# A convolution gate that stays in PSUM, and an output bias added in four slices during the mixer

## The chip, the cores and the metric

The kernel runs on one core of a Trainium2 chip, in one launch. The metric is the device time of one execution in microseconds (us); the median over the runs counts. The engines named here are PE (TensorE; PEld is its weight load), DVE (VectorE), ACT (ScalarE), POOL (GpSimd) and SP (SyncE, which only issues DMAs here).

## The reference

A decoder trunk of two layers over 256 tokens with 2048 features, all in float32. Layer 0 mixes tokens with a Conformer convolution, layer 1 with a diagonal state-space model (SSM); each mixer is followed by an MLP with a squared ReLU, and a last RMSNorm ends it. What matters here is the convolution mixer:

```python
def conv_module(h, w_in, b_in, dw, dw_b, ln_g, ln_b, w_out, b_out):
    u = h @ w_in + b_in                      # 2048 -> 4096
    a, gate = jnp.split(u, 2, axis=-1)
    v = a * jax.nn.sigmoid(gate)
    v = depthwise_causal_conv(v, dw, 31 taps) + dw_b
    v = layer_norm(v, ln_g, ln_b)
    v = jax.nn.silu(v)
    return v @ w_out + b_out                 # added to the residual x
```

## The kernel before

Every matmul is done in float32 quality with rounded operands: a weight tile `raw` is split into `hi` (ACT, L117) and `lo = raw - hi` (L119), and products of high and low parts are added up in PSUM. One weight tile (a step) is split in two halves; `run_steps` splits four halves ahead of the one that PE consumes, out of four buffers each for `hi` and `lo`. In the mixer's first projection (`conv_in`) DVE makes the `lo` of the first steps and POOL all the others (`pool_lo`), because DVE has the convolution to do.

`conv_in` walks over 16 blocks `c` of 128 channels. For each, PE computes value and gate rows (feature-major, 128 x 256 each) in one PSUM accumulator of two banks (`acc`, two buffers), over two steps, that is four halves of 24 matmuls (L204 to L206). Then `gate(c, A)` makes three instructions: DVE multiplies both by the RMSNorm factor of each token (L424, result `ga` in SBUF), ACT takes the sigmoid of the second half in place (L425), and DVE adds the bias to the first half and multiplies (L426, result in `vT`, SBUF).

For blocks 0 to 11 the depthwise convolution follows on DVE: one tap after another, 30 instructions of the form `scalar_tensor_tensor` (L792) into the PSUM tile `cv`, the last into `vT`. Blocks 12 to 15 (`PACKED`) are convolved on PE instead: a DMA (for block 15 copies on ACT and DVE, L445 and L447) lays out shifted rows `R`, POOL multiplies out the tap matrix `wpk` (L376), and 32 matmuls (L463, tile `pk`) give the block. For the LayerNorm, groups of blocks are centred by a common shift (L543), squared on ACT (L545) and summed over channels by PE (`stat`, L510); `ln_totals` and `ln_finish` (L555 to L579) finish the sums after block 15.

`ln_finish` then normalises block pair by block pair: DVE subtracts and scales (L792, L604), ACT applies SiLU (L607) and rounds the high part `sT` (L230), and DVE makes its low part (L231, both inputs in SBUF). PE multiplies `sT` by `w_out` (`conv_out`, L215 to L217) as soon as the pairs are there. The residual `x` lies in SBUF token-major; `add_x` adds each finished slice of 512 columns of `w_out`'s product to it.

Before the first step of `conv_out`, its `pre` calls `ln_finish`, then fetches the output bias as one tile `bo` (one row broadcast to 128 partitions, L624, on POOL's DMA queue) and adds it to `x` with four POOL instructions (L627). After that come the SSM's background preparations (`ssm_prep`), which begin with loads of `bb` on the same queue.

The order on each engine is made by a scheduler that simulates the program's times; `tick` and `after(n, fn)` place a function n halves later in the program, and `behind(ins)` keeps an instruction behind another. Where the text speaks of an order, it is the order in the built program.

Of the kernel before, what the change touches and what calls it, by code (L numbers as in the profile page):

```python
# [9 lines left out]
F32 = mybir.dt.float32  # L10
F32R = mybir.dt.float32r
I32 = mybir.dt.int32
AF = mybir.ActivationFunctionType
ALU = mybir.AluOpType
# [4 lines left out]
P = 128  # L19
EPS = 1e-6  # L20
D = 2048
T = 256
KB = D // P
NB = T // P
NS = D // 512
# [11 lines left out]
class Trunk:  # L37
# [320 lines left out]
    def packed_taps(self):  # L358

        nc = self.nc  # L360
        n = len(PACKED)
        self.R = self.blk_tile([P, 3, 4, T + 28], name="R")
        self.wpk = self.blk_tile([P, n, 32, 32], name="wpk")

        def prep():
            dp = self.t2([P, n, 4, 8], name="dp")
            for r in range(4):
                for g in range(4):
                    nc.vector.tensor_copy(out=dp[32 * r:32 * r + 32, :, g, :],
                                          in_=self.dw[32 * g:32 * g + 32, PACKED[0]:, r::4])  # L370
            for i in range(n):
                self.after(1 + 8 * i, lambda i=i: block(dp[:, i], i))

        def block(dp, i):
            with self.behind(self.pool_ins):
                nc.gpsimd.tensor_tensor(  # L376
                    out=self.wpk[:, i], in0=dp.rearrange("p g q -> p (g q)").unsqueeze(2).broadcast_to([P, 32, 32]),
                    in1=self.m32.unsqueeze(1).broadcast_to([P, 32, 32]), op=ALU.mult)
        self.after(16, prep)

    def behind(self, ins):
        return self.tc.issue_after(getattr(ins, "ins", ins))
# [36 lines left out]
    def gate(self, c, A):  # L419
        nc = self.nc  # L420
        b_in = self.vec("b_in")
        t = self.tmp.tile([P, 2, T], F32, tag="ga", name="ga", bufs=2)
        with self.tc.high_priority(offset=URGENT):
            nc.vector.tensor_tensor(out=t, in0=A, in1=self.rstdB.broadcast_to([P, 2, T]), op=ALU.mult)  # L424
            nc.scalar.activation(t[:, 1, :], t[:, 1, :], AF.Sigmoid, bias=b_in[:, KB + c:KB + c + 1])  # L425
            nc.vector.scalar_tensor_tensor(out=self.cblk(c), in0=t[:, 0, :], scalar=b_in[:, c:c + 1], in1=t[:, 1, :],  # L426
                                           op0=ALU.add, op1=ALU.mult)
        if c in PACKED:
            self.depthwise_packed(c)
        else:  # L430
            self.depthwise(c)
# [183 lines left out]
    def conv_out(self):  # L615
        w = self.a["conv_w_out"][0]
        st = {}

        def pre():
            self.flush()  # L620
            self.ln_finish()
            self.rate = 2.75
            bo = self.blk_tile([P, D], name="bo")
            self.nc.gpsimd.dma_start(out=bo, in_=self.a["conv_b_out"].broadcast_to([P, D]))  # L624
            for n in range(NS):
                s = slice(n * 512, (n + 1) * 512)
                self.nc.gpsimd.tensor_tensor(out=self.x[:, :, s], in0=self.x[:, :, s],  # L627
                                             in1=bo[:, s].unsqueeze(1).broadcast_to([P, NB, 512]), op=ALU.add)
            self.ssm_prep()
        for n in range(NS):  # L630
            for kc in range(4):
                def consume(hi, lo, half, n=n, kc=kc):
                    if half == 0 and kc == 0:
                        st["acc"] = self.acc2()
                        if n == 0:
                            st["ssq"] = self.new_ssq()
                            self.new_hT()
                    k0 = (kc % 2) * 4 + half * 2
                    self.mm_t(st["acc"], lambda kk: self.sT[kc // 2][:, k0 + kk], hi, lo,
                              kc == 0 and half == 0, kc == 3 and half == 1)  # L640
                    if n == NS - 1 and kc == 2:
                        self.rate = 0
                    if kc == 3 and half == 1:
                        self.add_x(st["acc"], n)
                        self.feed(n, st["ssq"], "mlp0")
                if n == 0 and kc < 2:
                    self.pool_lo.add(len(self.steps))
                self.add_t(w, kc * 4, n * 512, consume, pre if n == 0 and kc == 0 else None)
# [811 lines left out]
```

## Time and profile before

| | us |
|---|---|
| median of 3 runs | 2077.03 |
| lowest, highest | 2071.52, 2077.48 |
| the profiled execution | 2073.18 |
| its span in the trace | 2071.4 |
| PE, DVE, ACT, POOL busy in it | 1996.2, 1426.4, 942.6, 304.4 |

The profile is that of one execution; all durations come from it. Its own time is 1.8 us over its span and 3.9 us under the median. Busy shares are averages over stages that differ: the mixer lies in the first 260 us, the first MLP and the SSM's preparations behind it. Matmuls are pipelined, so that "busy" for PE counts overlapping times, and the number of matmuls in a stretch says more. In the timelines a group's duration spans from its first start to its last end.

### The profile page before, as it was taken

The numbers are of one execution on the slowest core, as the hardware profiler recorded it, in microseconds if no ns is written. First come the engines' busy times: TensorE is split into PE (matmuls) and PEld (weight loads), VectorE is DVE, ScalarE is ACT, GpSimd is POOL, SyncE is SP. The second block draws the span as 40 slices with busy tenths as digits, with TensorE's granted clock in tenths as the row PEclk, the third lists the DMA queues.
The fourth block names the chain that finished last, engine by engine and source line by source line (L and its number), as shares of the span: only waits on it lengthen the run. The fifth ranks groups of instructions, "written<-read, shape, count | busy, mean of one in ns | idle before, by whom it ended". The sixth has DMA issues, their size and how long they took to land.

```text
span 2071.4 us, 28883 instructions
## 1 busy us (share of the span) xinstructions
PE 1996.2 (96%) x11612; PEld 1696.8 (82%) x11612; DVE 1426.4 (69%) x1897; ACT 942.6 (46%) x1155; POOL 304.4 (15%) x234
## 2 busy tenths in 40 slices
PE   8999798999999999999987799999999999999998
PEld 8899587788888888888876588888888888888887
DVE  7999899966767777776548635566565555655555
ACT  5444454454444545444433244455344444544444
POOL 2987401100000211111013410000000000000000
PEclk9999999999999999999997999999999999999999
DMA  8667367766856876667999975666566566565663
GB/s 230 164 176 209 108 201 246 229 216 189 266 185 188 220 217 214 202 213 225 254 299 222 216 234 184 192 184 193 184 189 197 183 189 197 183 211 192 186 192 133
DMA packets 330485, 420.09 MB, mean 203 GB/s; under 512 B 10081, under 2 KB 228241, under 8 KB 327889
## 3 DMA queue, kind: packets, MB, share of 16 engines
q1 hardware_dynamic: 316864, 384.86, 62.8%
q0 software_dynamic: 9488, 29.02, 4.7%
q10 hardware_dynamic: 4000, 4.38, 0.7%
q8 instruction: 91, 1.49, 0.3%
q14 instruction: 42, 0.34, 0.0%
HBM read 391.69 MB, written 26.53 MB: 202 GB/s over the span
## 4 chain that ended last, share of the span: by engine, by line
PE 79%; DVE 12%; DMA 4%; SPq 1%; issue 1%; ACT 1%; POOL 1%; ACTq 0%; POOLq 0%; DVEq 0%
PE acc L194 22%; PE acc L215 14%; PE acc L216 14%; PE acc L217 14%; PE acc L195 11%; DVE cv L792 6%; DMA raw<-in_ssm_w_glu_dram 2%; DVE lo L119 1%; SPq L91 1%; DVE vT L426 1%; DVE ws L783 1%; DMA raw<-in_mlp_w_down_dram 1%; DMA Vt<-Vd 0%; PE acc L204 0%; PE acc L205 0%
## 5 line engine op out<-in xcount | busy, mean ns | idle before, releaser
L117 ACT ACTIVATE hi<-raw 128x1024 fp32r<-128x1024 f32 x672 | 711.0, 1060 | 983.7 <-PE acc L217 480.0
L119 DVE TENSOR_TENSOR lo<-raw,hi 128x1024 fp32r<-128x1024 f32 x596 | 729.3, 1224 | 534.5 <-ACT hi L117 533.5
L194 PE MATMUL acc<-hT,hi 128*128 128x512 f32 x2048 | 726.5, 399 | 3.4 <-DVE t L771 3.4
L195 PE MATMUL acc<-hT,lo 128*128 128x256 f32 x2048 | 575.3, 281 | 3.3 <-DVE lo L119 3.3
L194 PEld LDWEIGHTS acc<-hT,hi 128*128 128x128 f32 x2048 | 385.3, 188 | 100.0 <-issue 3.2
L215 PE MATMUL acc<-hi,rT 128*128 128x512 f32 x992 | 388.6, 392 | 6.2 <-ACT hi L117 6.2
L195 PEld LDWEIGHTS acc<-hT,lo 128*128 128x128 f32 x2048 | 387.5, 189 | 4.8 <-DVE lo L119 3.9
L216 PE MATMUL acc<-lo,rT 128*128 128x512 f32 x992 | 387.4, 391 | 0.5 <-DVE lo L119 0.5
L217 PE MATMUL acc<-hi,rT 128*128 128x512 f32 x992 | 387.0, 390 | 0.0
L215 PEld LDWEIGHTS acc<-hi,rT 128*128 128x128 f32 x992 | 186.8, 188 | 47.2 <-ACT hi L117 6.6
L217 PEld LDWEIGHTS acc<-hi,rT 128*128 128x128 f32 x992 | 186.8, 188 | 39.5
L216 PEld LDWEIGHTS acc<-lo,rT 128*128 128x128 f32 x992 | 186.7, 188 | 39.0 <-DVE lo L119 1.0
L119 POOL TENSOR_TENSOR lo<-raw,hi 128x1024 fp32r<-128x1024 f32 x76 | 187.3, 2482 | 115.4 <-ACT hi L117 106.6
L204 PE MATMUL acc<-hT,hi 128*128 128x256 f32 x512 | 146.0, 285 | 1.5 <-ACT hi L117 1.5
L206 PE MATMUL acc<-hT,lo 128*128 128x256 f32 x512 | 145.4, 284 | 1.9 <-POOL lo L119 1.9
L205 PE MATMUL acc<-hT,hi 128*128 128x256 f32 x512 | 146.1, 286 | 0.2 <-DVE hT L252 0.2
L792 DVE SCALAR_TENSOR_TENSOR cv<-vT,dw,cv 128x256 f32<-128x256 f32 x348 | 142.1, 478 | 0.8
L217 PE MATMUL acc<-hi,yT 128*128 128x512 f32 x256 | 101.3, 396 | 8.1 <-DVE yT L231 8.1
L783 DVE TENSOR_TENSOR x<-x,acc 128x1024 f32<-128x1024 f32 (+1 forms) x72 | 83.6, 1161 | 33.3 <-PE acc L217 22.9
L204 PEld LDWEIGHTS acc<-hT,hi 128*128 128x128 f32 x512 | 98.5, 192 | 4.1 <-ACT hi L117 2.1
L215 PE MATMUL acc<-hi,yT 128*128 128x512 f32 x256 | 101.6, 397 | 0.0
L206 PEld LDWEIGHTS acc<-hT,lo 128*128 128x128 f32 x512 | 98.5, 192 | 3.0 <-POOL lo L119 2.1
(264 smaller groups left out, 1759.1 us busy)
## 6 DMA issues: line engine op xcount, KB each, us to landing
raw<-in_mlp_w_up_dram SPq DMA_DIRECT2D x128, 1024.0 KB, 5.8
raw<-in_mlp_w_down_dram SPq DMA_DIRECT2D x128, 1024.0 KB, 5.2
raw<-in_ssm_w_glu_dram SPq DMA_DIRECT2D x32, 1024.0 KB, 5.6
raw<-in_conv_w_in_dram SPq DMA_DIRECT2D x60, 512.0 KB, 5.5
raw<-in_conv_w_out_dram SPq DMA_DIRECT2D x16, 1024.0 KB, 5.3
Vd<-bv POOLq DMA_DIRECT2D x16, 512.0 KB, 5.0
Wt<-Wd SPq DMA_DIRECT2D x8, 1024.0 KB, 9.8
Mt<-Kd SPq DMA_DIRECT2D x32, 256.0 KB, 14.1
```

The costliest lines, as they stand in the source:

```text
L117: self.nc.scalar.activation(hi, sl, AF.Copy)
L119: ins = eng.tensor_tensor(out=lo, in0=sl, in1=hi.bitcast(F32), op=ALU.subtract)
L194: mm(accs[m], lhsT=hi[:, kk, c], rhs=x, start=first and kk == 0, stop=False)
L195: mm(accs[m][:, 0:T], lhsT=lo[:, kk, c], rhs=x[:, 0, :], start=False, stop=last and kk == 3)
L204: mm(accs[m], lhsT=hi[:, kk, c], rhs=x[:, 0, :], start=first and kk == 0, stop=False)
L205: mm(accs[m], lhsT=hi[:, kk, c], rhs=x[:, 1, :], start=False, stop=False)
L206: mm(accs[m], lhsT=lo[:, kk, c], rhs=x[:, 0, :], start=False, stop=last and kk == 3)
L215: mm(acc[:, b, :], lhsT=ak[:, 0, t], rhs=hi[:, kk, :], start=first and kk == 0, stop=False)
L216: mm(acc[:, b, :], lhsT=ak[:, 0, t], rhs=lo[:, kk, :], start=False, stop=False)
L217: self.mm_last = mm(acc[:, b, :], lhsT=ak[:, 1, t], rhs=hi[:, kk, :], start=False, stop=last and kk == 1)
L783: self.nc.vector.tensor_tensor(out=out, in0=a, in1=b, op=op)
L792: return self.nc.vector.scalar_tensor_tensor(out=out, in0=a, scalar=s, in1=b, op0=op0, op1=op1)
```

## The change

Two edits. In `gate`, the scaled product overwrites the accumulator `A` in PSUM; ACT's sigmoid reads it there and writes a tile `ga` of half the size in SBUF, and the last DVE instruction reads the value half from PSUM and the sigmoid from SBUF. The accumulator is then read until this last instruction. The second edit takes the bias out of `conv_out`'s `pre` and puts it into the mixer: at ticks 20, 28, 36 and 44 after the taps are set up, one slice of 512 columns of the bias is fetched (a tile from the pool `t2`) and added to `x` by POOL, behind the `lo` instruction last issued there.

```diff
@@ packed_taps
         self.after(16, prep)
+        for i in range(NS):
+            self.after(20 + 8 * i, lambda i=i: self.add_b_out(i))
+
+    def add_b_out(self, n):
+        nc = self.nc
+        s = slice(n * 512, (n + 1) * 512)
+        bo = self.t2([P, 512], name="bo")
+        nc.gpsimd.dma_start(out=bo, in_=self.a["conv_b_out"][:, s].broadcast_to([P, 512]))
+        with self.behind(self.pool_ins):
+            nc.gpsimd.tensor_tensor(out=self.x[:, :, s], in0=self.x[:, :, s],
+                                    in1=bo.unsqueeze(1).broadcast_to([P, NB, 512]), op=ALU.add)
@@ gate
-        t = self.tmp.tile([P, 2, T], F32, tag="ga", name="ga", bufs=2)
+        t = self.tmp.tile([P, T], F32, tag="ga", name="ga", bufs=2)
         with self.tc.high_priority(offset=URGENT):
-            nc.vector.tensor_tensor(out=t, in0=A, in1=self.rstdB.broadcast_to([P, 2, T]), op=ALU.mult)
-            nc.scalar.activation(t[:, 1, :], t[:, 1, :], AF.Sigmoid, bias=b_in[:, KB + c:KB + c + 1])
-            nc.vector.scalar_tensor_tensor(out=self.cblk(c), in0=t[:, 0, :], scalar=b_in[:, c:c + 1], in1=t[:, 1, :],
+            nc.vector.tensor_tensor(out=A, in0=A, in1=self.rstdB.broadcast_to([P, 2, T]), op=ALU.mult)
+            nc.scalar.activation(t, A[:, 1, :], AF.Sigmoid, bias=b_in[:, KB + c:KB + c + 1])
+            nc.vector.scalar_tensor_tensor(out=self.cblk(c), in0=A[:, 0, :], scalar=b_in[:, c:c + 1], in1=t,
                                            op0=ALU.add, op1=ALU.mult)
@@ conv_out, pre
             self.flush()
             self.ln_finish()
             self.rate = 2.75
-            bo = self.blk_tile([P, D], name="bo")
-            self.nc.gpsimd.dma_start(out=bo, in_=self.a["conv_b_out"].broadcast_to([P, D]))
-            for n in range(NS):
-                s = slice(n * 512, (n + 1) * 512)
-                self.nc.gpsimd.tensor_tensor(out=self.x[:, :, s], in0=self.x[:, :, s],
-                                             in1=bo[:, s].unsqueeze(1).broadcast_to([P, NB, 512]), op=ALU.add)
             self.ssm_prep()
```

On POOL, the stretch from the second tap matrix `wpk` (L376) to the first loads of the SSM's preparations stood like this before; `lo` (L119) is the low part of a weight half, `rstd` the LayerNorm's factor, `x` the residual:

```order
L376 TENSOR_TENSOR wpk<-dp,m_244 128x1024
L119 TENSOR_TENSOR lo<-raw,hi 128x1024 x8
L376 TENSOR_TENSOR wpk<-dp,m_244 128x1024
L119 TENSOR_TENSOR lo<-raw,hi 128x1024 x8
L376 TENSOR_TENSOR wpk<-dp,m_244 128x1024
L119 TENSOR_TENSOR lo<-raw,hi 128x1024 x24
L587 TENSOR_TENSOR rstd<-lv,mhalf 128x2
L624 DMA bo<-in_conv_b_out_dram 128x2048
L839 DMA bb<-in_ssm_b_re_dram 128x1024
L840 DMA bb<-in_ssm_b_im_dram 128x1024
L627 TENSOR_TENSOR x<-x,bo 128x2x512 x4
```

The same engine in the changed kernel, from the same `wpk` on, down to the last bias DMA:

```order
L376 TENSOR_TENSOR wpk<-dp,m_244 128x1024
L119 TENSOR_TENSOR lo<-raw,hi 128x1024 x3
L388 DMA bo<-in_conv_b_out_dram 128x512
L119 TENSOR_TENSOR lo<-raw,hi 128x1024 x2
L388 DMA bo<-in_conv_b_out_dram 128x512
L390 TENSOR_TENSOR x<-x,bo 128x2x512
L119 TENSOR_TENSOR lo<-raw,hi 128x1024 x2
L390 TENSOR_TENSOR x<-x,bo 128x2x512
L388 DMA bo<-in_conv_b_out_dram 128x512
L119 TENSOR_TENSOR lo<-raw,hi 128x1024
L376 TENSOR_TENSOR wpk<-dp,m_244 128x1024
```

The four DMAs and four additions now stand among the mixer's `lo` instructions (the last DMA follows after one more `lo`, the third addition after two more; the fourth after another five `lo`, the last `wpk` and three `lo`); behind `rstd` the loads of `bb` follow at once.

On DVE, the end of the mixer before, from the gate of the last block (L424) to the last packed block's result; `cv` and `vT<-vT,dw,cv` are taps, `R` the copies for block 15, `shift` the centring of a group:

```order
L424 TENSOR_TENSOR ga<-acc,bcs 128x512
L792 SCALAR_TENSOR_TENSOR cv<-vT,dw,cv 128x256 x3
L426 SCALAR_TENSOR_TENSOR vT<-ga,vecs 128x256
L792 SCALAR_TENSOR_TENSOR cv<-vT,dw,cv 128x256 x2
L447 COPY R<-vT 32x284 x6
L792 SCALAR_TENSOR_TENSOR cv<-vT,dw,cv 128x256 x6
L792 SCALAR_TENSOR_TENSOR vT<-vT,dw,cv 128x256
L792 SCALAR_TENSOR_TENSOR cv<-vT,dw,cv 128x256 x3
L543 TENSOR_TENSOR vT<-vT,shift 128x3x256
L792 SCALAR_TENSOR_TENSOR vT<-vT,dw,cv 128x256
L543 TENSOR_TENSOR vT<-vT,shift 128x4x256
L792 SCALAR_TENSOR_TENSOR vT<-pk_2827,vecs,shift 128x256
```

The same place in the changed kernel:

```order
L798 SCALAR_TENSOR_TENSOR cv<-vT,dw,cv 128x256 x18
L798 SCALAR_TENSOR_TENSOR vT<-vT,dw,cv 128x256
L798 SCALAR_TENSOR_TENSOR cv<-vT,dw,cv 128x256
L436 TENSOR_TENSOR acc<-acc,bcs 128x2x256
L798 SCALAR_TENSOR_TENSOR vT<-vT,dw,cv 128x256
L555 TENSOR_TENSOR vT<-vT,shift 128x4x256
L438 SCALAR_TENSOR_TENSOR vT<-acc,vecs,ga 128x256
L459 COPY R<-vT 32x284 x6
L555 TENSOR_TENSOR vT<-vT,shift 128x3x256
L798 SCALAR_TENSOR_TENSOR vT<-pk_2839,vecs,shift 128x256
```

Of the 16 instructions for taps that stood behind the last gate's first instruction, one is left, and the centring of four blocks stands ahead of the gate's last instruction. On PE, the sums of blocks 8 to 11 moved with it, in among the products of block 14.

## Rows read from the trace of the kernel before

**Rows 1.** The page's head: span, and busy time, share and number of instructions of each engine, and the group of the high parts (count | busy us, mean ns of one | idle before, cause).

```profile
span 2071.4 us, 28883 instructions
...
PE 1996.2 (96%) x11612; PEld 1696.8 (82%) x11612; DVE 1426.4 (69%) x1897; ACT 942.6 (46%) x1155; POOL 304.4 (15%) x234
...
L117 ACT ACTIVATE hi<-raw 128x1024 fp32r<-128x1024 f32 x672 | 711.0, 1060 | 983.7 <-PE acc L217 480.0
```

**Rows 2.** Busy time by stretch (from:to, length; busy us and instructions of PE, PEld, DVE, ACT, POOL; granted PE clock, DMA share, GB/s): the mixer's middle, its end with `conv_out`'s begin, and the stretch behind that.

```profile
100.00:200.00 100.00, 100.00 (x837) 97.22 (x836) 95.59 (x207) 44.71 (x52) 86.11 (x36) 1.00 0.68 182
200.00:300.00 100.00, 89.15 (x659) 69.43 (x658) 88.20 (x196) 50.49 (x83) 27.23 (x18) 0.95 0.50 158
300.00:400.00 100.00, 92.61 (x482) 77.52 (x481) 99.15 (x142) 47.24 (x61) 13.07 (x8) 0.98 0.75 231
```

**Rows 3.** DVE's timeline over one block of the mixer (start us, us, line, operation; in brackets idle time before and its cause).

```profile
152.74 0.68 DVE L424 TENSOR_TENSOR ga<-acc,bcs 128x512 f32<-128x512 f32 x1
153.34 1.76 DVE L792 SCALAR_TENSOR_TENSOR cv<-vT,dw,cv 128x256 f32<-128x256 f32 x4
155.01 1.50 DVE L426 SCALAR_TENSOR_TENSOR vT<-ga,vecs 128x256 f32<-128x256 f32 x1
156.43 7.92 DVE L792 SCALAR_TENSOR_TENSOR cv<-vT,dw,cv 128x256 f32<-128x256 f32 x20
164.27 0.68 DVE L424 TENSOR_TENSOR ga<-acc,bcs 128x512 f32<-128x512 f32 x1
```

**Rows 4.** DVE's instructions from 45 to 218 us by line and form (count | busy us, mean ns | idle before, cause), and the line L426 over the whole run (duration ns min/median/max, first and last start us).

```profile
L792 DVE SCALAR_TENSOR_TENSOR cv<-vT,dw,cv 128x256 f32<-128x256 f32 x334 | 135.9, 478 | 0.6
L426 DVE SCALAR_TENSOR_TENSOR vT<-ga,vecs 128x256 f32<-128x256 f32 x15 | 21.5, 1433 | 1.0 <-ACT ga L425 1.0
L792 DVE SCALAR_TENSOR_TENSOR vT<-vT,dw,cv 128x256 f32<-128x256 f32 x10 | 4.6, 472 | 0.0
...
L426 DVE SCALAR_TENSOR_TENSOR vT<-ga,vecs x16: 476/1548/2427, 33.4 to 217.9; 128x256 f32<-128x256 f32 x16
```

**Rows 5.** POOL's timeline, four places (columns as in rows 3): a tap matrix and a `lo` in the steady stretch, the bias DMA, and the four additions of the bias.

```profile
144.67 2.09 POOL L376 TENSOR_TENSOR wpk<-dp,m 128x1024 f32<-128x1024 f32 x1
...
156.68 2.41 POOL L119 TENSOR_TENSOR lo<-raw,hi 128x1024 fp32r<-128x1024 f32 x1 [0.45 <-ACT hi L117]
...
238.06 0.64 POOL L624 DMA_DIRECT2D bo<-in_conv_b_out_dram  x1
...
243.29 9.71 POOL L627 TENSOR_TENSOR x<-x,bo 128x1024 f32<-128x1024 f32 x4 [3.55 <-DMA bo<-in_conv_b_out_dram]
```

**Rows 6.** PE's timeline at the mixer's end: the last matmul of block 15, the products of blocks 13 and 14, those of block 15, the last channel sums, and the LayerNorm's totals.

```profile
215.29 0.28 PE L206 MATMUL acc<-hT,lo 128*128 128x256 f32 x1
215.50 7.11 PE L463 MATMUL pk<-R,wpk 128*32 128x256 f32 x128
223.84 4.38 PE L463 MATMUL pk<-R,wpk 128*32 128x256 f32 x64 [1.22 <-DVE R L447]
231.04 1.08 PE L510 MATMUL stat<-vT,ones 128*32 128x256 f32 x8 [2.82 <-DVE vT L543]
...
234.97 1.06 PE L561 MATMUL lst<-q,stat 128*128 128x1 f32 x8 [0.50 <-ACT stat L555]
```

**Rows 7.** DVE's timeline: a centring of four blocks in the mixer, and the mixer's end.

```profile
193.26 2.25 DVE L543 TENSOR_TENSOR vT<-vT,shift 128x1024 f32<-128x1024 f32 x1
...
216.11 0.68 DVE L424 TENSOR_TENSOR ga<-acc,bcs 128x512 f32<-128x512 f32 x1
...
217.89 2.09 DVE L426 SCALAR_TENSOR_TENSOR vT<-ga,vecs 128x256 f32<-128x256 f32 x1
...
220.69 3.34 DVE L447 COPY R<-vT 32x284 f32<-32x284 f32 x6
...
228.38 0.95 DVE L543 TENSOR_TENSOR vT<-vT,shift 128x768 f32<-128x768 f32 x1
...
229.75 1.23 DVE L543 TENSOR_TENSOR vT<-vT,shift 128x1024 f32<-128x1024 f32 x1
```

**Rows 8.** ACT's timeline at the mixer's end: the copies for block 15, a table load, and the result of block 14.

```profile
220.01 4.05 ACT L445 ACTIVATE R<-vT 32x284 f32<-32x284 f32 x9 [2.67 <-DVE vT L426]
...
225.03 1.28 ACT L449 ACT_TABLE_LOAD   x1
...
226.44 0.46 ACT L471 ACTIVATE vT<-pk,vecs 128x256 f32<-128x256 f32 x1
```

**Rows 9.** DVE's timeline in `ln_finish`: the low parts of `sT`, the first two pairs of instructions and a later single one.

```profile
243.59 4.86 DVE L231 TENSOR_TENSOR sT<-z,sT 128x256 fp32r<-128x256 f32 x2
...
250.76 3.40 DVE L231 TENSOR_TENSOR sT<-z,sT 128x512 fp32r<-128x512 f32 x2
...
257.01 0.68 DVE L231 TENSOR_TENSOR sT<-z,sT 128x512 fp32r<-128x512 f32 x1
```

**Rows 10.** PE's timeline at the begin of `conv_out`: two matmuls that waited for `sT`, one of the slow ones behind the last wait, and one after those.

```profile
245.99 0.50 PE L217 MATMUL acc<-hi,sT 128*128 128x512 f32 x1 [1.97 <-DVE sT L231]
...
253.62 0.50 PE L217 MATMUL acc<-hi,sT 128*128 128x512 f32 x1 [3.44 <-DVE sT L231]
...
255.73 0.63 PE L217 MATMUL acc<-hi,sT 128*128 128x512 f32 x1
...
258.73 0.39 PE L217 MATMUL acc<-hi,sT 128*128 128x512 f32 x1
```

## The prediction

> **What bounds the kernel now.** I read the page's head first: PE is busy for nearly the whole span, no other engine is near it [rows 1]. But busy shares average over stages, so the stretches come next [rows 2]. From 100 to 200 us PE gets 837 matmuls done and POOL and DVE are at 86 and 96 of 100 us; from 200 to 300 us PE gets only 659 done, and loses 10.9 us outright. So the change, which touches the mixer and its end, is worth what it does to that second stretch, unless it slows the first.
>
> In the mixer the gate's first instruction comes every 11.53 us (152.74, 164.27) [rows 3]: that is PE's pace, four halves of 2.88 us. DVE has no idle time there either, but its work is merely late: what it has not done when PE ends block 15 at 215.5 us is done afterwards. There the reader should follow PE [rows 6]: products of blocks 13 and 14 at once, those of 15 at 223.84 after its copies, then nothing until DVE's centring lets the sums begin at 231.04; the totals come at 234.97. Behind that, PE waits for the low parts of `sT`: the pairs that DVE starts at 243.59 and 250.76 take 4.86 and 3.40 us [rows 9], and PE's waits end at 245.99 and 253.62 [rows 10].
>
> **The gate.** The same instruction, 128 x 256, takes 1.43 us on average at L426 but 0.476 us at its fastest; taps of the same form and size, with one input in PSUM, take 0.478 and 0.472 us, however busy POOL is [rows 4]. What differs is that L426 has both inputs in SBUF while POOL, which reads SBUF, runs. The changed instruction has one in PSUM, so I price it like the taps: 0.47 us, or 0.40 from start to start (20 taps in 7.92 us [rows 3]). Over 15 gates DVE saves 15 x (1.43 - 0.47) = 14.4 us of duration. The first one now writes PSUM: a tap that writes PSUM costs 0.006 us more than one that writes SBUF [rows 4], so 0.1 us for 16. No row has such an output of 512 columns; bounds by the taps' difference scaled to size are 0 to 0.012 us each, by an outright second tap 0.47 us each, 7.5 us in all, and I take the first.
>
> The row of L426 shows no price of a PSUM input. The Trainium skill (Perfetto Trace Analysis, Optimizing Scalar/DVE Operations) gives VectorE some 60 ns of access overhead on SBUF and 125 ns on PSUM; by that the gate's two instructions would lose 16 x 2 x 65 ns = 2.1 us, an estimate from that page, all within the reserve worked out below. The trace does not agree: 0.472 us with PSUM, 0.476 without.
>
> The accumulator is held longer, from the first gate instruction's end to the last's, 155.01 + 1.50 - 153.42 = 3.1 us before [rows 3] and about 2 us after. PE needs that buffer again a whole block (11.5 us) later: hidden, unless DVE is 8 us late, when PE would lose the difference.
>
> **What the saving is worth.** Not 14 us: PE sets the pace up to 215.5 us. Until then DVE was some 16 taps late, 14 `cv` and two `vT` by the built order, 16 x 0.39 = 6.3 us. The nine gates from about 105 us on give back 9 x (1.55 - 0.40) = 10.4 us at L426's median [rows 4], so that DVE is up to date with about 4 us in reserve, as the built order has it (one tap left behind the last gate's first instruction). I lay out the new end with the old durations, from PE's end at 215.5:
> - gate 215.7 to 216.3, one tap, centring of four blocks 2.25 (POOL still runs; 1.23 when it does not) [rows 7] to 219.0, last gate instruction to 219.4;
> - ACT squares that group (128 x 1024 as for `hi`, 1.06 [rows 1]) and then makes ten copies (9 in 4.05 us, the tenth apart [rows 8]): to 224.4, so block 15's products start about 224, not earlier than now;
> - block 14's result follows a table load of 1.28 us, at 226.4 or a little before [rows 8]; but DVE is now free and centres its group at once, done at 227.5 instead of 229.3;
> - eight fewer sums of blocks 8 to 11 stand at the end. The rest of block 15's products and the last six sums end near 229.0, the totals follow at 229.5 instead of 234.97 [rows 6].
>
> Gain 5.4 us; between 3.5, if the copies come a us or two late, and 6.5.
>
> **The bias.** Before, the tile has landed 5.2 us after its issue (238.06 to 243.29) and POOL adds for 9.71 us from 243.29 to 253.0 [rows 5], exactly over both slow pairs of `sT`. These have two inputs in SBUF; a later one of twice the first ones' size takes 0.68 us [rows 9]. With POOL idle there the first pair costs 2 x 0.45 = 0.9 and the second 2 x 0.65 = 1.3: 4.0 + 2.1 = 6.1 us. PE's resumption moves with it: from 253.62 to about 247.5, before the gain of the stage ahead. Then the granted clock: behind the wait eight matmuls or so stand at 0.63 us against 0.39 later, 0.43 and 0.23 from start to start (255.73, 258.73 [rows 10]), the lower and the higher of the clock's two levels, after PE had waited 3.44 us. With shorter waits up to 8 x 0.2 = 1.6 us come back; I take 1.0, as the stretch behind is partly DVE's.
>
> On the row of `sT` the Trainium skill bears (SBUF — State Buffer, Who interferes with whom): a VectorE instruction with two SBUF inputs and a GpSimd instruction that reads SBUF exclude each other for the whole length of the one that started first. By that rule the pairs are slow only through POOL, the sum is -6.1; were they slow on their own account it would be 0, and the time that of the second rival. The trace agrees: L217's wait ends at 245.99, when the first addition of 2.43 us (243.29 + 2.43 = 245.72) is over. The rule also speaks against the change, because the additions now meet the mixer's centrings; these pay up to 2.43 us each, within the reserve.
>
> **What the bias costs where it is now.** POOL gets four additions of 9.71 / 4 = 2.43 us and four issues of 0.64 (the whole tile's; a quarter may be cheaper): 12.3 us, between two tap matrices of 2.09 us [rows 5], from about 105 to 165 us. Its reserve: a half lasts 2.88 us, a `lo` 2.41, so 0.47 per half, 9.4 us over 20 halves. That leaves 12.3 + 2 x 2.09 - 9.4 = 7.1 us of backlog. The buffers carry part: a half is split when the buffers four halves back come free, three halves (8.6 us) ahead of use; less 1.06 for `hi` [rows 1] and 2.41 for `lo`, 5.2 us. PE should lose 1 to 2 us, spread over two places; nothing if sums on PE give POOL room, and, as the upper bound, all 12.3 us if POOL had no reserve. I take 1.0. Behind a late `lo` on POOL's queue stand only further `lo`, tap matrices and bias slices; for the `lo` PE waits. The slices' DMAs bring the same 1 MB as before, at 182 GB/s of other traffic [rows 2], each two `lo` ahead of its addition: hidden if landing takes the 5.2 us of the whole tile. On that queue the loads of `bb` come about 6 us earlier. That costs nothing; DVE's two multiplications of `bb` move in front of the last low parts of `sT`, which still come about 1 us before PE needs them. Without that cover PE loses 1 us.
>
> **Sum.** -5.4 - 6.1 - 1.0 + 1.0 = -11.5 us. From 300 to 400 us DVE is full [rows 2], with the same work, begun as much earlier; I see nothing there that gives the gain back. Against the profiled execution's 2073.2 us that is 2061.7, against the median of the runs, 3.9 us higher, 2065.5. I forecast 2064, its own range 2057 to 2070.
>
> **Rivals.**
> 1. *POOL becomes the mixer's bound; slower.* Each addition waits for its slice on POOL's queue as the first did before (3.55 us [rows 5]), and nothing else runs there. Then 4 x 3.55 = 14.2 us join the 7.1 of backlog; less 5.2 that the buffers carry, PE loses 16 us and more when DVE's centrings hold POOL too. With 4 us of the tail's gain gone as well: -11.5 - 1.0 + 16 + 4 = +7.5, about 2083. It decides once POOL is over 5.2 us late. For it: POOL's 86 of 100 us. Against: two `lo`, 4.8 us, lie between most DMAs and their additions. 8%.
> 2. *Only one of the two gains comes.* The gate stays slow, or the copies for block 15 and block 14's result, whose times hardly move, set the end; or the `sT` pairs are slow for another reason. Then about -5 - 1 + 1 = -5 us: 2070. For it: the copies begin no earlier in my layout. Against: PE's empty 2.82 us before the sums [rows 6] are waited for DVE alone. 14%.
> 3. *The gain comes and is lost again* by 400 us, where DVE is 99% busy and the scheduler's order differs from before: 2074 to 2076, no change. Against: DVE's work is no larger, and it starts earlier. 12%.
>
> My forecast has the other 66%. A measurement here cannot tell less than 0.3%, about 6 us, from no change: below 2070.8 is faster. Of rival 2 half lies there, of the forecast nearly all: faster 0.71, same 0.21, slower 0.08. The range 2055 to 2075 holds the forecast, rival 2 and part of rival 3.
>
> **What would show it.** Right: the gate's last instruction at 0.47 us throughout; PE without gaps over 2 us in all from 100 to 215 us; channel sums done about 5 us earlier; no `sT` low part over 1 us; POOL empty behind the LayerNorm's factor. Wrong: PE waiting for POOL's `lo` for many us between 105 and 170; the end of the sums still near 234; or PE ahead by 11 us at 300 and not at 450.

## The result, and the profile after

The changed kernel takes 2062.26 us, median of 9 runs (2056.67 to 2065.76), against 2075.69 for the kernel before in the same session (9 runs): ratio 0.9941, 95% interval 0.9921 to 0.9961, which is 12.2 us less (13.4 between the two medians). The forecast was 2064, range 2055 to 2075. The profiled execution took 2065.76 us, span 2063.8. Its lines are numbered otherwise: the gate's instructions are L436 to L438 (before L424 to L426), the taps L798, the centring L555, the products L475, the totals L573.

The stretches of [rows 2] after the change (same columns):

```profile
100.00:200.00 100.00, 99.86 (x833) 96.38 (x835) 93.39 (x224) 44.31 (x53) 93.70 (x44) 1.00 0.74 198
200.00:300.00 100.00, 98.08 (x725) 78.73 (x718) 83.38 (x197) 55.98 (x92) 20.73 (x14) 0.98 0.52 165
300.00:400.00 100.00, 93.85 (x495) 79.64 (x494) 100.00 (x138) 48.65 (x61) 9.56 (x9) 0.97 0.75 235
```

From 200 to 300 us PE gets 725 matmuls done instead of 659 and loses 1.9 us instead of 10.9. POOL has gone from 86.1 to 93.7 busy us in the mixer's middle, and PE hardly notices.

The gate's instructions (DVE groups from 45 to 218 us as in [rows 4]; last, the whole run's min/median/max in ns):

```profile
L436 DVE TENSOR_TENSOR acc<-acc,bcs 128x512 f32<-128x512 f32 x14 | 9.7, 694 | 7.5 <-PE acc L206 7.4
L438 DVE SCALAR_TENSOR_TENSOR vT<-acc,vecs,ga 128x256 f32<-128x256 f32 x14 | 6.7, 478 | 1.0 <-ACT ga L437 1.0
...
L438 DVE SCALAR_TENSOR_TENSOR vT<-acc,vecs,ga x16: 472/477/485, 34.4 to 222.5; 128x256 f32<-128x256 f32 x16
```

The last instruction has gone from 476/1548/2427 ns to 472/477/485, beside a POOL that does more. DVE also waits for PE again (7.5 us before L436).

The mixer's end on DVE (timeline; compare [rows 7]) and on PE (compare [rows 6]):

```profile
218.04 0.70 DVE L436 TENSOR_TENSOR acc<-acc,bcs 128x512 f32<-128x512 f32 x1 [1.42 <-PE acc L206]
...
219.15 3.43 DVE L555 TENSOR_TENSOR vT<-vT,shift 128x1024 f32<-128x1024 f32 x1
222.50 0.47 DVE L438 SCALAR_TENSOR_TENSOR vT<-acc,vecs,ga 128x256 f32<-128x256 f32 x1
...
241.90 0.75 DVE L231 TENSOR_TENSOR sT<-z,sT 128x256 fp32r<-128x256 f32 x2
...
244.96 1.28 DVE L231 TENSOR_TENSOR sT<-z,sT 128x512 fp32r<-128x512 f32 x2
```

```profile
217.93 4.08 PE L475 MATMUL pk<-R,wpk 128*32 128x256 f32 x70
...
227.80 3.67 PE L475 MATMUL pk<-R,wpk 128*32 128x256 f32 x52 [0.41 <-ACT R L457]
...
233.63 1.12 PE L573 MATMUL lst<-q,stat 128*128 128x1 f32 x8 [0.49 <-ACT stat L567]
...
245.70 0.50 PE L217 MATMUL acc<-hi,sT 128*128 128x512 f32 x1 [0.21 <-DVE sT L231]
```

Block 15 ends at 217.93 and the totals begin 15.70 us later (before 19.47). PE's 2.82 us of waiting ahead of the sums is gone. But the centring of four blocks takes 3.43 us and holds the last gate instruction until 222.50. Both `sT` pairs are short, and of PE's waits for them [rows 10] 0.21 us is left.

### The profile page after: what moved, and what is told of

Same layout as the page of the kernel before. It is cut to its first block, busy times and chain, and to the rows that moved or that the text cites. A ratio compares the mean times of both kernels' runs of the same rounds, so it can differ in the third digit from the quotient of the medians.

```text
span 2063.8 us, 28887 instructions
## 1 busy us (share of the span) xinstructions
PE 1998.9 (97%) x11612; PEld 1700.7 (82%) x11612; DVE 1404.7 (68%) x1897; ACT 942.3 (46%) x1155; POOL 298.6 (14%) x237
## 4 chain that ended last, share of the span: by engine, by line
PE 87%; DMA 4%; SPq 3%; DVE 3%; issue 1%; POOL 1%; ACT 1%; ACTq 0%; POOLq 0%; DVEq 0%
PE acc L194 23%; PE acc L215 14%; PE acc L217 14%; PE acc L216 14%; PE acc L195 12%; SPq L91 3%; PE acc L204 2%; PE acc L206 2%; PE acc L205 2%; DMA raw<-in_conv_w_in_dram 1%; DMA raw<-in_mlp_w_down_dram 1%; DVE lo L119 1%; DMA raw<-in_ssm_w_glu_dram 1%; DMA Mt<-Kd 1%; POOL lo L119 1%
## 5 line engine op out<-in xcount | busy, mean ns | idle before, releaser
L119 DVE TENSOR_TENSOR lo<-raw,hi 128x1024 fp32r<-128x1024 f32 x596 | 728.4, 1223 | 530.5 <-ACT hi L117 529.9
L195 PE MATMUL acc<-hT,lo 128*128 128x256 f32 x2048 | 575.3, 281 | 0.3 <-DVE lo L119 0.3
L195 PEld LDWEIGHTS acc<-hT,lo 128*128 128x128 f32 x2048 | 387.7, 189 | 1.5 <-DVE lo L119 0.6
L119 POOL TENSOR_TENSOR lo<-raw,hi 128x1024 fp32r<-128x1024 f32 x76 | 185.1, 2453 | 110.2 <-ACT hi L117 110.1
L798 DVE SCALAR_TENSOR_TENSOR cv<-vT,dw,cv 128x256 f32<-128x256 f32 x348 | 141.6, 481 | 0.7
L789 DVE TENSOR_TENSOR x<-x,acc 128x1024 f32<-128x1024 f32 (+1 forms) x72 | 83.5, 1160 | 33.9 <-PE acc L217 23.4
```

What stands on the lines that cost most here:

```text
L119: ins = eng.tensor_tensor(out=lo, in0=sl, in1=hi.bitcast(F32), op=ALU.subtract)
L195: mm(accs[m][:, 0:T], lhsT=lo[:, kk, c], rhs=x[:, 0, :], start=False, stop=last and kk == 3)
L789: self.nc.vector.tensor_tensor(out=out, in0=a, in1=b, op=op)
L798: return self.nc.vector.scalar_tensor_tensor(out=out, in0=a, scalar=s, in1=b, op0=op0, op1=op1)
```

## The experiments

To compare traces by stage, five marks are read from each: the end of block 15 on PE, the start of the totals (`lst`), and the first, fifth and 31st addition `x<-x,acc` of 128 x 1024 on DVE (L783 before, L789 after). The 31st, at 1028.12 us before, lies ahead of the SSM stage. The first three numbers are an instant and two distances from the mark before; "ratio" is the timed ratio to the kernel before.

| kernel | block 15 ends | to totals | to 1st add | 1st to 5th | 31st add at | ratio |
|---|---|---|---|---|---|---|
| before | 215.5 | 19.5 | 42.2 | 180.2 | 1028.1 | 1 |
| changed | 217.9 | 15.7 | 33.9 | 177.8 | 1016.1 | 0.9941 |
| changed, again | 215.4 | 15.7 | 33.9 | 177.8 | 1013.5 | 0.9940 |
| gate alone | 215.1 | 15.5 | 36.9 | 179.8 | 1018.0 | 0.9977 |
| slices alone | 235.4 | 15.9 | 33.1 | 177.8 | 1032.9 | 1.0045 |
| changed, no addition | 215.0 | 16.7 | 33.7 | 177.9 | 1014.1 | 0.9916 |
| before, no addition | 215.5 | 20.2 | 33.7 | 178.0 | 1018.1 | 0.9948 |
| slices, sigmoid in PSUM | 215.1 | 15.7 | 33.2 | 178.5 | 1013.3 | 0.9934 |

Between the two executions of the changed kernel 2.5 us lie ahead of the end of block 15: the first began its first gate 0.55 us later and ran at a granted clock of 0.97 from 45 to 100 us, the second at 1.00.

### One edit at a time

**The gate alone.** The kernel before, with the diff's lines in `gate` only:

```diff
+t = self.tmp.tile([P, T], F32, tag="ga", name="ga", bufs=2)
+nc.vector.tensor_tensor(out=A, in0=A, ...)
+nc.scalar.activation(t, A[:, 1, :], AF.Sigmoid, ...)
...
```

> The gate's edit alone; the bias is added where it was before. Theory 1 (the prediction's terms, one by one): the gate's last instruction goes from 1.43 to 0.47 us on average, DVE is up to date when PE ends block 15, and the whole gain of the tail comes with it: PE's end of block 15 to the totals falls from 19.5 us (234.97 - 215.50) to about 14, the sT pairs stay at 4.9 and 3.4 us, and the time falls by about 5 us (ratio 0.9975). Theory 2 (the queue's order and the gate's speed act only together): the built order of DVE's queue at the mixer's end is that of before, with eleven taps and both centrings behind the last gate; only the last gate instruction (2.09 to 0.47 us) gets shorter there and the spared time becomes DVE's waiting for PE, so the tail falls by 1 to 3 us, and the time by 1 to 3. Theory 3 (an instruction that writes 512 columns of PSUM and the longer hold of the accumulator cost as much as they save): no gain, PE waits for the accumulator between 100 and 215 us.

0.9977 (0.9962 to 0.9991), 2068.99 us median: theory 1's time, but not its tail. Theory 3 is out: no wait for the accumulator from 100 to 215 us. The tail falls by 4.0 us, though the built order of DVE's queue is the old one, with eleven taps and both centrings behind the last gate. So most of the tail's gain needs no new order. Not all of it is safe without one, though: with the same gate and the same old order, but PE's last sums partly at the lower clock, the tail is 16.2 to 16.7 us in three further kernels below (granted clock 0.57 from 227 to 231 us in one of them, 1.00 with the gate alone). And the distance to the first addition falls by 5.2 us, which neither theory had: the first `sT` pair now begins at 237.95, ahead of POOL's additions at 238.56 (before, 243.59 and 243.29), and takes 0.76 us, so that only the second is slow, and PE waits 2.8 us for `sT` instead of 6.3.

**The slices alone.** The kernel before, with the slices in the mixer and the old gate:

```diff
+for i in range(NS):
+    self.after(20 + 8 * i, lambda i=i: self.add_b_out(i))
```

> The bias slices alone; the gate is that of before, with its last instruction at about 1.4 us. Theory 1 (terms one by one): -6.1 at the sT pairs, -1.0 clock, +1.0 for POOL in the mixer, so about -6 us (ratio 0.997); the tail from PE's end of block 15 to the totals stays near 19.5 us. Theory 2 (the two edits act only together): the built order now puts every tap of blocks 13 and 14 and one centring ahead of the last gate's last instruction; with the slow gate DVE arrives there 5 to 8 us late, the tail stays as long or gets up to 3 us longer, and the time falls by 3 to 6 us. Rival 1 of the prediction (POOL is the mixer's bound): PE loses over 5 us between 105 and 215 us, and the time does not fall.

1.0045 (1.003 to 1.0061), 2082.38 us: slower than before by some 9 us. All that the slices remove behind the mixer is there (rows of the table), but block 15 ends 19.9 us late. One instruction of the old gate (DVE, timeline):

```profile
133.14 17.39 DVE L438 SCALAR_TENSOR_TENSOR vT<-ga,vecs 128x256 f32<-128x256 f32 x1
```

POOL over the same stretch, and PE's waits from 100 to 215 us (us in total, times, longest):

```profile
129.45 4.78 POOL L119 TENSOR_TENSOR lo<-raw,hi 128x1024 fp32r<-128x1024 f32 x2
134.19 2.40 POOL L390 TENSOR_TENSOR x<-x,bo 128x1024 f32<-128x1024 f32 x1
136.56 11.81 POOL L119 TENSOR_TENSOR lo<-raw,hi 128x1024 fp32r<-128x1024 f32 x5
148.34 1.90 POOL L376 TENSOR_TENSOR wpk<-dp,m 128x1024 f32<-128x1024 f32 x1
164.92 4.73 POOL L119 TENSOR_TENSOR lo<-raw,hi 128x1024 fp32r<-128x1024 f32 x2 [14.68 <-ACT hi L117]
```

```profile
PE acc L204 <- ACT hi L117: 17.2, 1, 17.2
```

The instruction ends at 150.53, 0.29 us after POOL's first pause (148.34 + 1.90 = 150.24). DVE's queue then runs its 29 taps before the next gate's first instruction; ACT's sigmoid waits 19.58 us for that, with the `hi` of the next halves behind it in ACT's queue, and PE waits for `hi`. POOL, which caused it, then stands still for 14.68 us. Of the 19.9 us PE's wait is 17.2; behind it the granted clock is 0.86 from 163 to 185 us, where the kernels without this wait have 1.00.

This instruction is the exception in its own trace. Another of the same line also came while POOL went from one instruction to the next without a pause, and was done 0.28 us after the end of the one that was running (DVE, then POOL, timeline):

```profile
175.05 1.07 DVE L438 SCALAR_TENSOR_TENSOR vT<-ga,vecs 128x256 f32<-128x256 f32 x1
```

```profile
173.44 2.40 POOL L390 TENSOR_TENSOR x<-x,bo 128x1024 f32<-128x1024 f32 x1
175.80 12.09 POOL L119 TENSOR_TENSOR lo<-raw,hi 128x1024 fp32r<-128x1024 f32 x5
```

Here the gate's instruction was let in between two POOL instructions, and five `lo` took 12.09 us; beside the 17.39 us, where none was let in, five took 11.81.

### Is it the shared port?

**One operand moved.** By the shared port is meant what the prediction describes: a DVE instruction with two inputs in SBUF and a POOL instruction that reads SBUF exclude each other. The edit is the slices alone, and the sigmoid written into the accumulator's second half instead of SBUF.

```diff
-nc.scalar.activation(t[:, 1, :], t[:, 1, :], AF.Sigmoid, ...)
-nc.vector.scalar_tensor_tensor(out=self.cblk(c), in0=t[:, 0, :], ..., in1=t[:, 1, :],
+nc.scalar.activation(A[:, 1, :], t[:, 1, :], AF.Sigmoid, ...)
+nc.vector.scalar_tensor_tensor(out=self.cblk(c), in0=t[:, 0, :], ..., in1=A[:, 1, :],
```

> The bias slices alone, with one operand moved: the sigmoid is written into the gate's second half of PSUM, so that the gate's last instruction has one input in SBUF and one in PSUM. The built order of DVE and of POOL is that of the slices alone, row for row. Theory of the shared port (an instruction with two SBUF inputs can't start while POOL runs, and POOL without a gap keeps it out): the last instruction takes 0.47 us, the one of 17.39 us is gone, PE loses nothing in the mixer, and the time is that of the changed kernel, 12 to 14 us faster than the slices alone (0.993 to 0.995 of the kernel before). Rival (the slices hold POOL back so far that PE waits for lo, whatever DVE does): PE still waits about 17 us once between 130 and 170 us, and the time stays near 1.0045.

0.9934 (0.9918 to 0.995), 2060.02 us: 22 to 23 us below the slices alone (by the medians, by the ratios), by one operand. The gate's last instruction over the run, with the slices alone and with the operand moved:

```profile
L438 DVE SCALAR_TENSOR_TENSOR vT<-ga,vecs x16: 473/1016/17390, 33.6 to 238.7; 128x256 f32<-128x256 f32 x16
```

```profile
L438 DVE SCALAR_TENSOR_TENSOR vT<-ga,vecs,acc x16: 468/476/482, 33.1 to 219.6; 128x256 f32<-128x256 f32 x16
```

PE waits for nothing from 100 to 215 us. POOL does the same work in the same order, now without a pause from 128.1 to 184.6 us. So the rival is out, and with it the thought that POOL's load is what costs. The gain was put too low (12 to 14 us).

**A pause per block.** The slices alone, with the old gate, and behind it on POOL a sum that needs the gate's result:

```diff
+j = self.small.tile([P, 2], F32, tag="gj", name="gj")
+nc.gpsimd.tensor_tensor(out=j, in0=self.cblk(c)[:, :2], in1=self.cblk(c)[:, 2:4], op=ALU.add)
```

> The bias slices alone with the old gate, and one tiny instruction more per block on POOL: the sum of two columns of the gate's result with two others, which POOL can't begin before the gate's last instruction is done, so that POOL pauses once per block. If the 17.39 us are a wait for POOL's first pause, no gate instruction takes over 3 us now, although POOL has more to do; PE's wait of 17.2 us goes, and the time falls by 8 to 13 us against the slices alone. Rival (the long instruction comes from POOL's amount of work): it stays over 10 us, and the time is no better.

0.9976 (0.9964 to 0.9989), 2069.0 us, 13 to 14 us below the slices alone although POOL does more. The longest gate instruction is 6.29 us, over the 3 us that were put down: the built order sets one addition and one `lo` ahead of the pause. It starts at 132.44 and POOL comes to rest at 138.44 (DVE's, then POOL's timeline):

```profile
132.44 6.29 DVE L438 SCALAR_TENSOR_TENSOR vT<-ga,vecs 128x256 f32<-128x256 f32 x1
```

```profile
133.69 2.40 POOL L390 TENSOR_TENSOR x<-x,bo 128x1024 f32<-128x1024 f32 x1
136.05 2.39 POOL L119 TENSOR_TENSOR lo<-raw,hi 128x1024 fp32r<-128x1024 f32 x1
138.81 0.19 POOL L441 TENSOR_TENSOR gj<-vT 128x2 f32<-128x2 f32 x1 [0.37 <-DVE vT L438]
```

It ends at 138.73, again 0.29 us after the pause began. PE's wait falls from 17.2 to 6.1 us. For this instruction the length follows the distance to POOL's pause, not POOL's load; why it was not let in at 133.72 or 136.09, between two POOL instructions, as the one at 175.05 was above, this does not show.

### How much room POOL and the changed kernel have

**Three times the additions.** The changed kernel, each slice added, subtracted, added.

```diff
+for op in (ALU.subtract, ALU.add):
+    nc.gpsimd.tensor_tensor(out=self.x[:, :, s], in0=self.x[:, :, s], in1=..., op=op)
```

> The changed kernel with every slice of the bias added, subtracted and added again on POOL (8 more instructions of 2.4 us, 19.2 us in all, in the mixer; the result is the same up to rounding). It asks how far POOL was from being the mixer's bound. By the prediction's working (backlog of 7.1 us, buffers for 5.2) PE waits for lo by 15 to 20 us more, and the time rises by as much against the changed kernel (1.001 to 1.004 of the kernel before). If POOL's reserve is larger than worked out (the changed kernel lost 0.4 us or less where 1.0 was put down), PE waits less than 10 us more. If POOL's longer stretch without a pause also reaches a centring of four blocks, that centring takes over 10 us, as the gate instruction did with the slices alone.

1.0074 (1.0054 to 1.0095), 2086.93 us, worse than any theory's number. PE's longest waits from 100 to 240 us, and the centring of blocks 4 to 7 on DVE:

```profile
PE stat L525 <- DVE vT L558: 11.8, 1, 11.8
PE acc L206 <- POOL lo L119: 8.7, 7, 2.9
```

```profile
184.33 11.80 DVE L558 TENSOR_TENSOR vT<-vT,shift 128x1024 f32<-128x1024 f32 x1
```

Two prices show. PE waits 8.7 us for `lo`, all of it before 180 us, where the prediction's working gave 15 to 20: POOL's reserve is larger than worked out. And the centring waits for POOL's pause at 195.04 as the old gate did in the slices alone, while PE, its sums next in the queue, waits with it. In the changed kernel POOL also runs on end, from 130.89 to 184.83; that same centring starts at 186.10, and in the second execution 1.3 us ahead of the stretch's end. It takes 2.4 us there. Whether it would have taken 11.80 further inside the stretch, as here, no run of the changed kernel shows.

**No addition at all**, in the changed kernel and in the one before:

```diff
-self.after(20 + 8 * i, lambda i=i: self.add_b_out(i))
```

> The changed kernel without the addition of the mixer's output bias (left out: conv_b_out is never added). So POOL has neither the slices in the mixer nor the additions behind it. If the slices in the mixer cost what the prediction said, this is 1 us faster than the changed kernel; if POOL's slices also hold DVE's centrings and delay the mixer by 2 to 4 us, it is that much faster. But if the slices are what brings the new order of DVE's queue at the mixer's end (the built order here is the old one: eleven taps and both centrings behind the last gate), the tail is 1 to 3 us longer than in the changed kernel, and the two effects about cancel: within 3 us of the changed kernel, with PE's end of block 15 about 1.5 us earlier.

> The kernel before without the addition of the mixer's output bias (left out: conv_b_out is never added); its gate is the old one. It prices the additions behind the mixer by themselves. The prediction: the sT pairs fall from 4.9 and 3.4 us to 0.8 and 1.4, PE resumes 6.1 us earlier and gets about 1.0 back through the clock, so about -7 us by 270 us; the tail is unchanged at 19.5 us. Were the pairs slow on their own account, they would stay at 4.9 and 3.4 us and the time would not fall.

Changed: 0.9916 (0.9893 to 0.9939). Block 15 ends 0.4 us earlier than in the second execution of the changed kernel, so the slices cost at most that; the tail is 1.0 us longer, its sums running partly at the lower clock (granted clock 0.66 from 227 to 232 us; 1.07 us for six of them, with the gate alone 0.61). The marks at the 31st addition differ by 0.6 us. Before: 0.9948 (0.9929 to 0.9967), about 11 us; to the first addition 8.5 us are gained, and another 2.3 between first and fifth. So the additions behind the mixer cost 10.8 us there, of which the changed kernel gets 8.3 + 2.4 (by the rounded marks).

### Other places for the work

**The centring later.** The changed kernel with the centring of blocks 8 to 11 behind DVE's copies, its square behind ACT's.

```diff
-self.after(2, lambda: self.centre(g[0], 4))
+self.after(2 if c < 8 else 99, lambda: self.centre(g[0], 4))
...
+with self.behind(self.rc_dve) if late else nullcontext():
```

> The changed kernel with the centring of blocks 8 to 11 put behind the last gate and DVE's copies of block 15 (and its square behind ACT's copies). If the centring of 3.43 us ahead of the last gate instruction is what holds the tail's gain at 3.8 us, the last gate instruction starts at 219.1 instead of 222.5, block 15's products at about 224.4 instead of 227.8, and the totals 2 to 4 us earlier than 233.6; the time falls by as much. Rival: the end is set by block 14's result and the centring of the last three blocks; then the totals move by less than 1 us.

0.9946 (0.9925 to 0.9967), beside 0.9940 (0.9919 to 0.9961) for the changed kernel on the same chip: no difference. The last gate instruction came at 218.21, 1.5 us behind block 15's end instead of 4.6, and the totals 15.0 us behind it instead of 15.7. The rival was nearer: PE has 192 products, 10.6 us, and 28 sums to do there, and it now waits for square and centring (0.9 us each) instead.

**The two kernels beside each other, and the additions held back.** With the same chip's runs, the changed kernel and the gate alone again; and twice the gate with the four additions behind `sT`: first behind the last high part in the order of issue, then with a tiny POOL instruction ahead that reads the last low part:

```diff
+v = self.sT[-1][:, 6:8, 1, 0:1].bitcast(F32)
...
+gj = self.nc.gpsimd.tensor_tensor(out=j, in0=v, in1=v, op=ALU.add)
+with self.behind(gj):
```

> The changed kernel once more, as the measure for the three kernels beside it. About 0.994 of the kernel before. Where its time behind the mixer's end differs between executions, it should do so behind 1000 us, and the first x<-x,acc should start within 1 us of 267.6 again, the one at 902.4 within 1 us too.

> The gate's edit alone once more, beside the changed kernel. If the trace of its first run is right that it has 10 of the 12 us by 905 us, it is 1 to 3 us slower than the changed kernel; if the first timing is right (0.9977 against 0.9941 of the kernel before), it is 7 us slower, and the difference must lie behind 1000 us, for between the mixer's end and there both do the same work.

> The gate's edit, and the bias added where the kernel before adds it but with the four additions held behind the last high part of sT, so that POOL is free while DVE makes the sT pairs; nothing is added in the mixer. If the additions' place over the sT pairs is all that the slices remove, and the slices cost 2 us in the mixer (the kernel without any addition is 2.0 us ahead at 900 us), this is 0 to 2 us faster than the changed kernel: sT pairs at 0.8 and 1.3 us, first x<-x,acc at about 265.5. Rival: the additions then meet DVE's x<-x,acc, which needs the summed residual, and these wait: slower than the changed kernel by up to 5 us.

> What the hold of the additions by order alone did not do: the gate's edit, and the four additions behind the mixer made to wait for DVE's last low part of sT (a tiny POOL instruction that reads it stands ahead of them). Nothing is added in the mixer. If the additions cost what they cost before only through their place over DVE's sT pairs, the pairs take 0.75 and 1.28 us, PE does not wait over 1 us for sT, and the first x<-x,acc comes near 263 us, 2 to 4 us ahead of the gate alone (267.2) and level with the changed kernel (264.95) or ahead; its time is then 0.994 or a little less of the kernel before. Rival: the additions, now over the end of conv_out's first columns, hold the first x<-x,acc and the next DVE instructions with two SBUF inputs, or POOL's later work comes later; then it is at 0.996 to 0.998, as the gate alone.

The changed kernel: 0.9940, the gate alone 0.9978 (0.9957 to 0.9998), as the first time. At the 31st addition the two are 1018.15 - 1013.53 = 4.6 us apart, less than the 7.5 us of their medians. The first hold held nothing (0.9964, 0.9946 to 0.9983): the order of issue made POOL wait for no other engine, and the additions began at 239.54, over the second pair. The second (0.998, 0.9965 to 0.9995) did free the pairs, 0.76 and 1.29 us, but the additions then lay from 263.57 to 274.03 and held up DVE's next instructions:

```profile
264.56 2.48 DVE L119 TENSOR_TENSOR lo<-raw,hi 128x1024 fp32r<-128x1024 f32 x1 [0.95 <-ACT hi L117]
...
267.52 4.16 DVE L796 SCALAR_TENSOR_TENSOR wk<-wk 128x1 f32<-128x1 f32 x2
...
275.55 1.21 DVE L787 TENSOR_TENSOR x<-x,acc 128x1024 f32<-128x1024 f32 x1
```

Two instructions on one column took 4.16 us. From the totals to the first addition it is 43.0 us again, as before the change. No free place was found behind the mixer. In the mixer from 45 us on, once the gate is changed, only the centrings have two inputs in SBUF.

## Why the prediction was right, and where it was not

The time was right, and the mechanism of each part; the sum was not built as the kernel behaves. That -11.5 met the 12.2 us is in part luck. The terms as measured below add up to about -14.4, which is what the second execution has at the 31st addition (-14.6); some 2 us of it do not show in the runs' ratio.

- **The gate's price** (1.43 to 0.47 us, by the second SBUF input): right, shown by the moved operand. L436 into PSUM takes 694 ns on average, before 681; the 0.012 us put as the bound is the 0.013 measured. By the overheads of the Trainium skill (Perfetto Trace Analysis, Optimizing Scalar/DVE Operations) that the prediction quoted, the last instruction had to take 0.065 us more than with SBUF alone, an estimate from that page. The trace does not agree: it takes 472 ns at its fastest, before 476.
- **The tail, -5.4:** measured -3.8, in the bounds of 3.5 to 6.5. The step mis-sized is the layout "centring of four blocks 2.25 ... to 219.0, last gate instruction to 219.4": that centring took 3.43 us. In the second execution, where block 15 ends at 215.4 as in the layout, it ended at 220.05 and ACT's copies at 225.7 instead of 224.4; "3.5, if the copies come a us or two late" was the right bound. With the centring out of the way the tail is 15.0 instead of 15.7, so it accounts for 0.7 of the 1.6 us that are short; the rest was not taken apart. That the new built order is needed for the gain was wrong: the gate alone keeps the old order and has 15.5 in both its executions.
- **`sT` -6.1 and clock -1.0:** measured 42.2 - 33.9 = 8.3 for both, by the mechanism given (before without additions: 8.5). But 5.2 of it come with the gate alone.
- **The slices, +1.0:** measured 0 to 0.4. POOL's reserve was underrated, and POOL did not wait for a slice.
- **"From 300 to 400 us ... I see nothing there that gives the gain back":** nothing was given back, but the sum has no term for the 2.5 us more that were gained between the first and the fifth addition. PE's waits for DVE's `lo` at L195 there fall from 3.3 to 0.4 us. The stretch takes 177.8 to 178.8 us where no additions stand behind the mixer (180.0 with three times the additions in it), and 178.5 to 180.2 where they do. DVE's queue is built in another order there; which of its rows does it was not tried.
- **"These pay up to 2.43 us each, within the reserve":** it held in size in the changed kernel, whose centrings took 2.17, 2.42 and 3.43 us, against 1.23 without POOL. As a bound it is wrong: 17.39, 6.29 and 11.80 us were waits for POOL's next pause and not for one instruction, in the slices alone, with a pause per block and with three times the additions. So the price of the slices beside the old gate, a loss of some 9 us, was not in the prediction. Nor do the edits add up: at the 31st addition the gate alone has -10, the slices alone +4.8, both -12.0 to -14.6. In the changed kernel no DVE instruction with two SBUF inputs falls into POOL's 54 us without a pause, except a centring near its end in one of the two executions; that the centrings lie there is luck, as the prediction did not place them against it.
- **Rivals.** The first did not come, but the slices alone show its price, PE's wait of 17.2 us, by another way than lateness of `lo`. The second and third are out: both gains come, and all of it is there at 1013 to 1016 us.

Behind the 31st addition the span has another 1043.3 us before, 1047.7 and 1045.4 after, 1039 to 1048 over all kernels; that stretch waits for DMAs, and I did not follow it. It stays open why the gate alone, 10 us ahead at that mark in both traces, is only 5 us faster by its runs. Its traced executions are its fastest and its second fastest (2061.0 and 2062.65 us, medians 2068.99 and 2070.03), so that its slower runs were not seen in a trace.

## What to carry to other kernels

Before giving a second engine more work, look for its pauses and not only for its share. A VectorE instruction with two inputs in SBUF waits here for the POOL instruction that is running, up to 2.4 us; and where POOL ran on end, three waited until its next pause, up to 17.39 us in all, with everything queued behind them. Move one operand into PSUM first, then fill POOL. And time two edits of one change apart: here one of them alone is slower than before, and the pair is faster than either.

## What was not expected of the hardware

The wait for the shared port is not always bounded by one instruction. The Trainium skill (SBUF — State Buffer, SBUF: two separate sides) has the exclusion last for the instruction that started first, which would be 2.4 us here. Most waits agree. From 20 to 300 us of the 14 traces, 87 gate, centring, `sT` and `lo` instructions of DVE with two SBUF inputs took over 0.15 us longer than alone. Of them 83 were done 0.3 us (gate) to 1.1 us (centring) after the end of the POOL instruction that was running; in 37 of these POOL's next addition, product or `lo` began without a pause, as at 175.05 above. A fourth missed one such end by 0.09 us and took the next. Three do not agree: 6.29, 11.80 and 17.39 us, over three, five and eight POOL instructions on end, and a release 0.29 us (gate) or 1.09 us (centring) after POOL's pause began.

What sets these three apart is open. They began 24 us and more into a stretch of POOL without a pause of 0.1 us, and that stretch held issues of bias DMAs. The 37 began 19.3 us into a stretch at the latest, and theirs held none. No run varies either alone.

It goes the other way too. POOL's `rstd` of 128 x 2, 0.70 us elsewhere, took 5.56 us in the kernel before at 361.36, while DVE ran these on end:

```profile
361.58 1.22 DVE L783 TENSOR_TENSOR wt<-bb,pw 128x1024 f32<-128x1024 f32 x1
362.72 1.22 DVE L783 TENSOR_TENSOR ws<-bb,pw 128x1024 f32<-128x1024 f32 x1
363.85 1.22 DVE L783 TENSOR_TENSOR wt<-bb,pw 128x1024 f32<-128x1024 f32 x1
364.99 0.22 DVE L783 TENSOR_TENSOR pw<-pw,wk 128x64 f32<-128x64 f32 x1
365.12 1.22 DVE L119 TENSOR_TENSOR lo<-raw,hi 128x1024 fp32r<-128x1024 f32 x1
366.26 0.48 DVE L252 SCALAR_TENSOR_TENSOR hT<-xt,vecs,hT 128x256 fp32r<-128x256 f32 x1
```

It ended at 366.92, behind the last of them. This was read once, not tried.
